# Projection steps spread over attention's rest, and two feed-forward weight pairs begun ahead of the last scale

## The chip, the cores and the metric

The kernel runs on one core of one Trainium2 chip. The metric is the device time of one execution, in microseconds; lower is better. A core has five engines that work at the same time and meet only through semaphores: PE (TensorE, matrix products; its weight loads are listed apart as PEld), DVE (VectorE), ACT (ScalarE), POOL (GpSimd) and SP (SyncE, which here only issues DMA transfers; POOL issues some too). Each engine works its own list of instructions in a fixed order.

## The reference, cut to what matters

The kernel computes one encoder layer for two request groups, a long one of 2048 tokens and a short one of 256, with the same weights. The model width is 1024, the feed-forward width 2816.

```python
h = rmsnorm(x, norm1_w)
p = h @ w_in
mq, mk, mv, mo, gates, aq, ak, av = jnp.split(p, cuts, axis=-1)
m_out = mlstm_mixer(mq, mk, mv, mo, gates, b_gates, mh_norm_w)
a_out = attention_mixer(aq, ak, av, q_norm_w, k_norm_w)
x = x + jnp.concatenate([m_out, a_out], axis=-1) @ w_out
h = rmsnorm(x, norm2_w)
u = centred_dwconv(h @ w_up, conv_w, conv_b)
a, g = jnp.split(u, 2, axis=-1)
return x + (jax.nn.silu(g) * a) @ w_down
```

The change touches the output projection (`@ w_out`), the second norm and the first products of `h @ w_up`.

## The kernel before, in words

Every fp32 operand of a product is split into a high part (an fp32r copy made by ACT) and a low part (the rest, made by DVE's subtraction), and each product is three matmuls: high by high, high by low, low by high. So nearly every operand costs an ACT copy and a DVE subtraction ahead of the matmuls that read it; the low part is read last.

The work runs in four stages. The first (`phase_a`) norms x and projects it. In the second, the mLSTM and the attention run side by side: `run_both` (L1481) holds a generator for each and takes the next step of whichever is behind by cost units. A step of attention scores 256 keys against 512 queries (L553, L554, tiles `ps`), ACT takes the exponent (L557, `pe`) and the high part (L558, `xx`), DVE the low part (L559), and PE multiplies with the values (L570, L571, L572 into `pv`; L572 is the one that reads the low part). The running maxima for the next head come from L530 (`px`) and DVE's L532 (`mx`). At a head pair's end ACT copies `pv` out (L580), DVE takes a reciprocal (L585), POOL multiplies (L586) and stores the outcome to `mix_d` in DRAM (L591).

When the mLSTM is through, `after_m` opens the memory of the third stage, `phase_c` (L906), which is a generator too: four steps that load and split the 16 half tiles of W_out (`wo`), then nine blocks of 256 tokens in the order `ORDER = (0, 1, 2, 3, 4, 5, 8, 6, 7)`, block 8 being the short sequence, each in eight steps. A block loads its mixed heads (`cmx`, L931 to L933), multiplies them with W_out (L945, tiles `po`, 192 matmuls of 256 columns a block), adds the residual (L952, tiles `cx`), squares (L955) and sums (L957, L960). One block later `tail` makes the scale: PE sums over partitions (L129, `rs_c`), DVE adds epsilon (L132, `rcol_c`), POOL takes the power (L133), PE spreads it over the partitions (L135), DVE scales the block in eight instructions (L964) and four DMAs store it to `n2_d` (L966); the last block's four stores go through POOL's queue, the others through SP's. `run_both` takes `CSTEP = 1` step of this generator ahead of every attention step, where the heads that the next block needs have been issued (`g.mixed`). The steps that are left when attention has ended are taken by the loop over `rest` in `body`, with the first loads of the feed-forward between them; the last block's scale is kept for `g.c_end()`.

The feed-forward (`phase_d`) multiplies in a seven-product scheme: for each pair of weight chunks (`UpPair`) the products "11", "21", "t2", "t1", "t3", "22", "t4" of quarter blocks, with sums of the weights (`w_sums`, L1055, tiles `tw`) and sums of the normed tokens (`nt`). "11" (into `pa`) and "21" (into `pb`) read the loaded weights (`wa`), the next two read `wb`, which is split from the sums `tw`. Token operands are loaded and split at L1020 to L1022 (`n`, `nt`): those of "11", "21", "t2" (`EARLY`) in the loop over `rest`, the other four (`LATE`), of two halves each, in `up_phase` at a raised priority, into memory that `wo` and the last `cmx` held. The first group's two pairs are number 22 and number 0: pair 22 has its "11" and "21" issued ahead of `g.c_end()`, pair 0 behind it, in `begin`.

The order of instructions on each engine is not the program's: a scheduler fixes it when the kernel is built, from the program, the priorities and the pools, so an edit of one stage moves instructions of its neighbours too.

## Time and profile before

| | us |
|---|---|
| three runs | 3367.17, 3370.07, 3371.93 |
| median | 3370.07 |
| the profiled execution | 3374.5 |
| its span, first to last instruction | 3372.8 |
| PE busy | 3265.6 (97%) |
| DVE busy | 2449.7 (73%) |
| ACT busy | 1993.7 (59%) |
| mLSTM's last products | about 1446 on the trace's clock |
| attention's last product | 1806.06 |
| last product of the projection | ends by 1868.64 |
| first product of the feed-forward with summed weights | 1890.39 |

A row of the timeline holds the start in us, the duration in us, engine, source line, operation, what it writes and reads, the number of instructions in the row, and in brackets how long the engine had been idle before it and what ended that. Matmuls overlap in the pipeline, so the time a matmul takes of PE is the distance from its start to the next one's start, not its duration. A row of the windows gives the length of a stretch, then for each engine its busy time and its instructions, then the granted TensorE clock (1.00 is full), the share of the DMA engines and what they moved. `PE L945` with `x1309` in a table by lines means 1309 matmuls of that line in the window.

### The profile page before, as it was taken

The page shows a single profiled execution, that of the slowest core. Times are in us where ns is not written, and L with a number is a line of the kernel's source. Part 1 is how long each engine was busy: PE and PEld are TensorE (multiplying, and loading weights), DVE is VectorE, ACT ScalarE, POOL GpSimd, SP SyncE. Part 2 cuts the span into 40 slices and gives each one's busy share as a digit, 9 for nine tenths or more (in the row PEclk, how much of TensorE's full clock was granted, in tenths as well). Part 3 has the DMA queues.
Part 4 walks back from the last instruction along what each step waited for, and adds up shares of the span by engine and source line. Part 5 has one row for each costly group of instructions (what it writes and reads, how often), then busy time and mean ns, then how long its engine had stood idle before and what let it go on. Part 6 is the DMA issues. An engine that isn't in the chain of part 4 may idle for free.

```text
span 3372.8 us, 53440 instructions
## 1 busy us (share of the span) xinstructions
PE 3265.6 (97%) x19566; PEld 3040.0 (90%) x19566; DVE 2449.7 (73%) x3659; ACT 1993.7 (59%) x3706; POOL 689.1 (20%) x1076
## 2 busy tenths in 40 slices
PE   7889999999999999999998899999999999999998
PEld 6778888888888888878887899999999999999998
DVE  7874576667657768876665799998889888666664
ACT  4535666666666766765454555676667667554543
POOL 7774033313225323211111100000000000010101
PEclk9999999999999999999999899999999999999999
DMA  8766243333236434423335666677666657867673
GB/s 245 214 182 180 91 137 94 108 106 112 94 107 206 133 123 129 142 89 107 97 97 175 242 210 218 215 249 263 240 224 240 212 195 262 312 225 276 226 241 117
DMA packets 393783, 601.69 MB, mean 178 GB/s; under 512 B 31248, under 2 KB 254512, under 8 KB 393520
## 3 DMA queue, kind: packets, MB, share of 16 engines
q1 hardware_dynamic: 360144, 552.38, 48.9%
q0 software_dynamic: 11920, 34.09, 3.7%
q10 hardware_dynamic: 21456, 11.80, 1.2%
q8 instruction: 154, 2.52, 0.3%
q14 instruction: 109, 0.89, 0.1%
HBM read 434.23 MB, written 163.92 MB: 177 GB/s over the span
## 4 chain that ended last, share of the span: by engine, by line
PE 55%; DMA 3%; issue 2%; DVE 2%; ACT 2%; POOL 1%; SPq 0%; POOLq 0%; DVEq 0%; ACTq 0%
PE pa L1097 16%; PE pc L1097 8%; PE pf L1354 5%; PE po L945 5%; PE pb L1097 4%; PE ph L1354 3%; PE pg L1354 2%; PE mv L711 1%; PE ps L553 1%; PE ps L554 1%; PE pv L570 1%; PE pv L572 1%; PE pv L571 1%; PE px L530 1%; DMA nt<-act_d 1%
## 5 line engine op out<-in xcount | busy, mean ns | idle before, releaser
L559 DVE TENSOR_TENSOR xx<-pe,xx 128x1024 fp32r<-128x1024 f32 x260 | 320.5, 1234 | 156.3 <-ACT xx L558 155.2
L557 ACT ACTIVATE pe<-ps 128x1024 f32<-128x1024 f32 x260 | 266.1, 1024 | 234.1 <-PE ps L554 227.1
L532 DVE TENSOR_REDUCE mx<-px 128x1 f32<-128x1024 f32 x256 | 310.1, 1218 | 115.4 <-PE px L530 115.0
L1312 POOL TENSOR_TENSOR sq<-sq,sq 128x384 f32<-128x384 f32 x38 | 49.4, 1300 | 1389.5 <-ACT sq L1308 1309.2
L558 ACT ACTIVATE xx<-pe 128x1024 fp32r<-128x1024 f32 x260 | 275.1, 1058 | 5.6
L945 PEld LDWEIGHTS po<-cmx,wo 128*128 128x128 f32 x1728 | 234.6, 193 | 35.2 <-ACT cmx L932 13.5
L945 PE MATMUL po<-cmx,wo 128*128 128x256 f32 x1728 | 243.2, 285 | 14.8 <-ACT cmx L932 12.7
L1101 ACT ACTIVATE u<-pa 128x386 f32<-128x386 f32 (+2 forms) x264 | 129.3, 490 | 174.4 <-PE pa L1097 173.3
L570 PE MATMUL pv<-xx,vv 128*128 128x512 f32 x520 | 212.1, 408 | 7.4 <-ACT xx L558 4.4
L553 PE MATMUL ps<-qq,kk 128*128 128x512 f32 x520 | 214.7, 413 | 4.5 <-ACT pe L557 3.9
L572 PE MATMUL pv<-xx,vv 128*128 128x512 f32 x520 | 210.8, 405 | 1.5 <-DVE xx L559 1.3
L554 PE MATMUL ps<-qm,kl 65*128 65x512 f32 x520 | 208.2, 400 | 0.0
L571 PE MATMUL pv<-xx,vl 128*64 128x512 f32 x520 | 208.2, 400 | 0.0
L685 PEld LDWEIGHTS mj<-mn,wm 128*128 128x128 f32 x1296 | 179.6, 193 | 18.9 <-ACT og L699 4.6
L685 PE MATMUL mj<-mn,wm 128*128 128x256 f32 x1296 | 193.1, 288 | 2.9 <-ACT og L699 2.5
L695 PE MATMUL mv<-wm,mn 128*128 128x256 f32 x1296 | 191.0, 287 | 2.7 <-ACT qb L691 2.5
L695 PEld LDWEIGHTS mv<-wm,mn 128*128 128x128 f32 x1296 | 177.3, 191 | 17.1 <-ACT qb L691 4.0
L227 PE MATMUL pj<-w_a,n1T 128*128 128x512 f32 (+1 forms) x864 | 179.3, 362 | 10.0 <-DVE n1T L185 6.7
L227 PEld LDWEIGHTS pj<-w_a,n1T 128*128 128x128 f32 x864 | 144.6, 196 | 30.1 <-DVE n1T L185 7.6
L530 PE MATMUL px<-kk,qq 128*128 128x512 f32 x512 | 165.6, 405 | 5.1 <-ACT pe L557 3.4
L789 ACT ACTIVATE dm<-dm,tm 128x128 f32<-128x128 f32 x288 | 95.9, 392 | 111.5 <-POOL dm L786 107.0
L1097 PE MATMUL pb<-n,wa 128*128 128x386 f32 (+2 forms) x792 | 147.5, 341 | 3.8 <-DVE cx L964 3.8
(326 smaller groups left out, 8316.1 us busy)
## 6 DMA issues: line engine op xcount, KB each, us to landing
mn<-n_d SPq DMA_DIRECT2D x216, 256.0 KB, 3.3
ru<-w_up SPq DMA_DIRECT2D x88, 512.0 KB, 5.2
rs<-wsu_d SPq DMA_DIRECT2D x88, 512.0 KB, 5.5
act_d<-ts SPq DMA_DIRECT2D x33, 768.0 KB, 5.8
nt<-act_d SPq DMA_DIRECT2D x60, 384.0 KB, 4.9
re_t<-wsd_d SPq DMA_DIRECT2D x45, 512.0 KB, 5.5
wsu_d<-tw SPq DMA_DIRECT2D x44, 512.0 KB, 4.2
act_d<-ya SPq DMA_DIRECT2D x99, 192.0 KB, 2.9
```

The lines of the kernel that those rows point to most:

```text
L227: nc.tensor.matmul(pjs[t][:, c0:c1], nTs[tiles[t]][:, c, a, :], ws[c][:, b, c0:c1], start=(c == 0 and k == 0), stop=(c == NCC - 1 and k == 2))
L532: nc.vector.tensor_reduce(s.mx[:, t0, z0:z0 + 1], ps, AX.X, ALU.max)
L553: nc.tensor.matmul(o, kk[:, kc:kc + P], s.qq, start=True, stop=False)
L557: nc.scalar.activation(pe, ps, AF.Exp)
L558: nc.scalar.activation(x[:, 0], pe, AF.Copy)
L559: nc.vector.tensor_tensor(x[:, 1], pe, f32(x[:, 0]), ALU.subtract)
L570: nc.tensor.matmul(s.pv, vv[:, kt % 4, :], x1, start=kt == 0, stop=False)
L685: nc.tensor.matmul(pj[:, o], s.w[c][:, a, o * P:(o + 1) * P], nT[c][:, h, :], start=(c + o + k == 0), stop=(c == NCC - 1 and k == 2 and o ...
L695: nc.tensor.matmul(pv[:, o], nT[c][:, a, o * P:(o + 1) * P], s.w[c][:, h, 256:512], start=(c + o + k == 0), stop=(c == NCC - 1 and k == 2 ...
L945: nc.tensor.matmul(po[:, o], wo[c][z // 2][:, a, n], mx[c][:, h, :], start=(c == 0 and k == 0), stop=(c == NCC - 1 and k == 2))
L1097: s.nc.tensor.matmul(p, w[:, aa, c, :], ops[k][:, c, bb, 0:s.n], start=c == 0 and i == 0 and not add, stop=c == NCC // 2 - 1 and i == 2, s ...
L1354: nc.tensor.matmul(ps[c], w[:, aa, c, :], t[:, gi - g0, bb, 0:H], start=gi == 0 and m == 0 and not more, stop=gi == NG - 1 and m == 2, ski ...
```

## The change

Three things change.

- `run_both` no longer takes a projection step ahead of every attention step. It counts the attention steps that are left when the mLSTM ends (`left`) and takes steps so that 52 of them (4 of weights and six blocks of eight, `CSTEPS`) are spread evenly over these; it never begins the seventh block of the order, the short sequence's block 8, so that this block's eight steps are issued after attention's last step. 
- The operands of "t1" and "t3" (`MID`) get a pool of their own, `d_m`, in the memory of the W_out halves 4 to 7. Those halves now lie in a stack of their own, which is closed ahead of `g.c_end()`; the loads of `MID` are issued there.
- Pair 0 also has its products "11" and "21" issued ahead of `g.c_end()`, into the same PSUM pool as pair 22's. The third PSUM tile of both pairs (`pc`) comes from the other pool.

Lines of the changed kernel from 81 to about 1480 have numbers that are lower by one: its L944 is L945 here, its L963 is L964.

```diff
-CSTEP = 1
+CSTEPS = 52
...
-EARLY, LATE = OPS[:3], OPS[3:]
+EARLY, MID, LATE = OPS[:3], OPS[3:5], OPS[5:]
...
-        s.g, s.nc, s.s1, s.ps, s.b, s.jj = g, g.nc, s1, ps, b, jj
+        s.g, s.nc, s.s1, s.ps, s.pc, s.b, s.jj = g, g.nc, s1, ps, ps, b, jj
...
-        return s.ps.tile([P, 512], F32, tag="p", name=f"p{k}_{s.nm}", bufs=PB)[:, 0:s.n]
+        return (s.pc if k == "c" else s.ps).tile([P, 512], F32, tag="p", name=f"p{k}_{s.nm}", bufs=PB)[:, 0:s.n]
...
-def phase_d(g, tc, s1, pd, ops, first):
+def phase_d(g, tc, s1, sm, pd, ops, first):
...
-        sl = st.enter_context(tc.tile_pool(name="d_l", bufs=1, side="right", reuse_waits="tile"))
+        sr = st.enter_context(tc.tile_pool(name="d_l", bufs=1, side="right", reuse_waits="tile"))
+        sl = {k: s1 if k in EARLY else sm if k in MID else sr for k in OPS}
...
-    late = n2_ops(sl, 0, LATE)
+    for p in first:
+        p.pc = banks[1]
     with tc.high_priority(offset=APRI):
-        for k, e in zip(LATE, P0):
-            n2_load(g, late, 0, k, engs=e)
-    ops.update(late)
+        for k in LATE:
+            ops.update(n2_ops(sl[k], 0, [k]))
+            n2_load(g, ops, 0, k)
...
     def begin(b, gi):
-        prs = [UpPair(g, s1, banks[0], b, 2 * gi + NFC)] if not first else [first.pop()]
-        prs.append(UpPair(g, s1, banks[1], b, 2 * gi))
-        for k, p in enumerate(prs):
-            if (b, gi, k) != (0, 0, 0):
-                p.mul(p.p1, "11", opsb[b])
-        for k, p in enumerate(prs):
-            if (b, gi, k) != (0, 0, 0):
-                p.second(opsb[b])
+        if (b, gi) == (0, 0):
+            return first
+        prs = [UpPair(g, s1, banks[k], b, 2 * gi + NFC * (1 - k)) for k in range(2)]
+        for p in prs:
+            p.mul(p.p1, "11", opsb[b])
+        for p in prs:
+            p.second(opsb[b])
         return prs
...
-                swo = pool(s_wo, "wo", bufs=1, side="right")
                 sc = pool(s_wo, "c_s", bufs=2, side="right")
                 pc = pool(s_wo, "c_p", bufs=2, space=PSUM, side="right")
+                g.s_sw = s_wo.enter_context(ExitStack())
+                swo = pool(g.s_sw, "wo", bufs=1, side="right")
...
             first[0].second(ops)
+            g.s_sw.close()
+            sm = pool(s2, "d_m", bufs=1)
+            with tc.high_priority(offset=APRI):
+                for k in MID:
+                    ops.update(n2_ops(sm, 0, [k]))
+                    n2_load(g, ops, 0, k)
+            first.append(UpPair(g, s1, pd, 0, 0))
+            first[1].mul(first[1].p1, "11", ops)
+            first[1].second(ops)
             g.c_end()
             s_wo.close()
-            phase_d(g, tc, s1, pd, ops, first)
+            phase_d(g, tc, s1, sm, pd, ops, first)
...
+    na_s, left, steps = 2 * (16 * 8 + 2), 0, 0
...
                 tile_c = next(c)
+                left = max(na_s, 1)
         else:
-            for _ in range(CSTEP):
-                if c is not None and (tile_c is None or tile_c in g.mixed):
-                    tile_c = next(c, NT)
+            if c is not None and steps * left < CSTEPS * (left - na_s) and tile_c != 2 * ORDER[6] and (
+                    tile_c is None or tile_c in g.mixed):
+                tile_c = next(c)
+                steps += 1
...
             da = None if s is None else da + s
+            na_s -= 1
```

The places in the order of instructions on which the prediction rests follow. First PE at the hand-over to the feed-forward, from the projection's last row to the first product with `wb` (`cacc7` and `rs_c7` are block 7's sums of squares, the kernel's last scale); before:

```order
L945 MATMUL po7_3_20911<-cmx7_7_20721,wo7_1_17285 128x256 x3
L1097 MATMUL pa_0_22_20970<-n11_0_20190,wa0_22_20967 128x386 x10
L1097 MATMUL pb_0_22_20983<-n21_0_20191,wa0_22_20967 128x386 x10
L129 MATMUL rs_c7_20997<-ones_82,cacc7_20799 128x2 x2
L135 MATMUL rs_c7_20997<-ident_73,rcol_c7_21000 128x128 x2
L1097 MATMUL pa_0_0_21071<-n11_0_20190,wa0_0_21068 128x386 x12
L1097 MATMUL pb_0_0_21084<-n21_0_20191,wa0_0_21068 128x386 x12
L1097 MATMUL pa_0_22_20970<-nt2_0_20192,wb0_22_21121 128x386 x2
```

After:

```order
L944 MATMUL po7_3_20911<-cmx7_7_20721,wo7_1_17321 128x256 x3
L1096 MATMUL pa_0_22_20970<-n11_0_20076,wa0_22_20967 128x386 x10
L1096 MATMUL pb_0_22_20983<-n21_0_20077,wa0_22_20967 128x386 x10
L1096 MATMUL pa_0_0_21019<-n11_0_20076,wa0_0_21016 128x386 x12
L1096 MATMUL pb_0_0_21032<-n21_0_20077,wa0_0_21016 128x386 x12
L128 MATMUL rs_c7_21046<-ones_82,cacc7_20799 128x2 x2
L134 MATMUL rs_c7_21046<-ident_73,rcol_c7_21049 128x128 x2
L1096 MATMUL pa_0_22_20970<-nt2_0_20078,wb0_22_21124 128x386 x2
```

Pair 0's 24 products have moved ahead of the two rows of the scale's sums. The row of `po7_3` above and the 342 matmuls of L945 from attention's last value product to it are as many as before, all of blocks 6 and 7 after one another; none of block 8 has moved there.

The same place on DVE, from the first split of late operands (`n22`, `nt1`, `nt3`, `nt4`; each row of one is half a tile) to the scale's last rows; before:

```order
L1022 TENSOR_TENSOR nt1_0_21035<-nt1_0_21035 128x2x386
L1104 TENSOR_TENSOR u0_22_21117<-pb_0_22_20983,u0_22_21117 128x386
L132 TENSOR_SCALAR rcol_c7_21000<-rs_c7_20997 128x2
L1022 TENSOR_TENSOR nt1_0_21035<-nt1_0_21035 128x2x386
L1022 TENSOR_TENSOR nt3_0_21036<-nt3_0_21036 128x2x386
L964 SCALAR_TENSOR_TENSOR cx7_0_20689<-cx7_0_20689,nw_84,rs_c7_20997 128x256 x2
L964 SCALAR_TENSOR_TENSOR cx7_1_20690<-cx7_1_20690,nw_84,rs_c7_20997 128x256 x2
L964 SCALAR_TENSOR_TENSOR cx7_2_20691<-cx7_2_20691,nw_84,rs_c7_20997 128x256
L1022 TENSOR_TENSOR nt3_0_21036<-nt3_0_21036 128x2x386
L964 SCALAR_TENSOR_TENSOR cx7_2_20691<-cx7_2_20691,nw_84,rs_c7_20997 128x256
L1022 TENSOR_TENSOR n22_0_21037<-n22_0_21037 128x2x386 x2
L1022 TENSOR_TENSOR nt4_0_21038<-nt4_0_21038 128x2x386
```

After:

```order
L1103 TENSOR_TENSOR u0_22_21120<-pb_0_22_20983,u0_22_21120 128x386
L1021 TENSOR_TENSOR n22_0_21083<-n22_0_21083 128x2x386
L1021 TENSOR_TENSOR nt4_0_21090<-nt4_0_21090 128x2x386
L1021 TENSOR_TENSOR nt1_0_21000<-nt1_0_21000 128x2x386 x2
L1103 TENSOR_TENSOR u0_0_21122<-pb_0_0_21032,u0_0_21122 128x386
L131 TENSOR_SCALAR rcol_c7_21049<-rs_c7_21046 128x2
L1021 TENSOR_TENSOR nt3_0_21007<-nt3_0_21007 128x2x386 x2
L963 SCALAR_TENSOR_TENSOR cx7_0_20689<-cx7_0_20689,nw_84,rs_c7_21046 128x256 x2
L963 SCALAR_TENSOR_TENSOR cx7_1_20690<-cx7_1_20690,nw_84,rs_c7_21046 128x256 x2
L963 SCALAR_TENSOR_TENSOR cx7_2_20691<-cx7_2_20691,nw_84,rs_c7_21046 128x256
L1021 TENSOR_TENSOR nt4_0_21090<-nt4_0_21090 128x2x386
L963 SCALAR_TENSOR_TENSOR cx7_2_20691<-cx7_2_20691,nw_84,rs_c7_21046 128x256
```

L132 (now L131) stood behind one split and one copy of pair 22 (`u0_22`); now five splits (the row ahead of this piece is the first, of `n22`), that copy and pair 0's `u0_0` stand ahead of it. Two more splits follow ahead of the first scale product, as before. Of the eight splits five stood among the scale products; now one does.

The third place is DVE in the middle of attention's rest, where the projection of block 4 (`po4_0`, `po4_1`) waits for the last of its mixed heads (`cmx4_7`) and block 3 is scaled (`cx3`). The tiles `xx4_12` are those of the attention head in work, the next figure numbering its eight passes over the keys (1, 2, 3 here), and `mx5_12` holds the maxima for the head that follows; before:

```order
L559 TENSOR_TENSOR xx4_12_1_18255<-pe4_12_1_18254,xx4_12_1_18255 128x1024
L132 TENSOR_SCALAR rcol_c3_19330<-rs_c3_19327 128x2
L532 TENSOR_REDUCE mx5_12_18195<-px5_12_2_0_18265 128x1
L532 TENSOR_REDUCE mx5_12_18195<-px5_12_3_0_18269 128x1
L964 SCALAR_TENSOR_TENSOR cx3_0_18743<-cx3_0_18743,nw_84,rs_c3_19327 128x256 x2
L964 SCALAR_TENSOR_TENSOR cx3_1_18744<-cx3_1_18744,nw_84,rs_c3_19327 128x256 x2
L964 SCALAR_TENSOR_TENSOR cx3_2_18745<-cx3_2_18745,nw_84,rs_c3_19327 128x256 x2
L933 TENSOR_TENSOR cmx4_7_19243<-cmx4_7_19243 128x256
L964 SCALAR_TENSOR_TENSOR cx3_3_18746<-cx3_3_18746,nw_84,rs_c3_19327 128x256 x2
L532 TENSOR_REDUCE mx5_12_18195<-px5_12_0_1_18360 128x1
L933 TENSOR_TENSOR cmx5_7_19685<-cmx5_7_19685 128x256
L559 TENSOR_TENSOR xx4_12_2_18344<-pe4_12_2_18343,xx4_12_2_18344 128x1024
```

After:

```order
L131 TENSOR_SCALAR rcol_c3_19356<-rs_c3_19353 128x2
L531 TENSOR_REDUCE mx5_12_18170<-px5_12_2_0_18236 128x1
L531 TENSOR_REDUCE mx5_12_18170<-px5_12_3_0_18240 128x1
L558 TENSOR_TENSOR xx4_12_1_18226<-pe4_12_1_18225,xx4_12_1_18226 128x1024
L963 SCALAR_TENSOR_TENSOR cx3_0_18769<-cx3_0_18769,nw_84,rs_c3_19353 128x256 x2
L963 SCALAR_TENSOR_TENSOR cx3_1_18770<-cx3_1_18770,nw_84,rs_c3_19353 128x256 x2
L963 SCALAR_TENSOR_TENSOR cx3_2_18771<-cx3_2_18771,nw_84,rs_c3_19353 128x256 x2
L963 SCALAR_TENSOR_TENSOR cx3_3_18772<-cx3_3_18772,nw_84,rs_c3_19353 128x256 x2
L531 TENSOR_REDUCE mx5_12_18170<-px5_12_0_1_18295 128x1
L558 TENSOR_TENSOR xx4_12_2_18279<-pe4_12_2_18278,xx4_12_2_18279 128x1024
L932 TENSOR_TENSOR cmx4_7_19269<-cmx4_7_19269 128x256
```

The low part of pass 1 stood ahead of the two maxima, now it stands behind them, next to the eight scale products. On PE the same stretch has, before, around the row that spreads the scale (L135):

```order
L571 MATMUL pv4_12_18423<-xx4_12_1_18255,vl1_16_0_10624 64x512
L572 MATMUL pv4_12_18423<-xx4_12_1_18255,vv1_16_0_10623 128x512
L570 MATMUL pv4_12_18423<-xx4_12_1_18255,vv1_16_0_10623 128x512
L571 MATMUL pv4_12_18423<-xx4_12_1_18255,vl1_16_0_10624 64x512
L572 MATMUL pv4_12_18423<-xx4_12_1_18255,vv1_16_0_10623 128x512
L135 MATMUL rs_c3_19327<-ident_73,rcol_c3_19330 128x128 x2
L553 MATMUL ps4_12_2_18338<-qq4_12_17721,kk1_16_4_10632 128x512
L554 MATMUL ps4_12_2_18338<-qm4_12_17723,kl11_16_4_10633 128x512
L553 MATMUL ps4_12_2_18338<-qq4_12_17721,kk1_16_4_10632 128x512
L554 MATMUL ps4_12_2_18338<-qm4_12_17723,kl11_16_4_10633 128x512
L530 MATMUL px5_12_0_1_18360<-kk1_16_8_10643,qq5_12_18191 128x512
L530 MATMUL px5_12_0_1_18360<-kk1_16_12_10654,qq5_12_18191 128x512
```

After, from that row on:

```order
L134 MATMUL rs_c3_19353<-ident_73,rcol_c3_19356 128x128 x2
L552 MATMUL ps4_12_2_18273<-qq4_12_17696,kk1_16_4_10632 128x512
L553 MATMUL ps4_12_2_18273<-qm4_12_17698,kl11_16_4_10633 128x512
L552 MATMUL ps4_12_2_18273<-qq4_12_17696,kk1_16_4_10632 128x512
L553 MATMUL ps4_12_2_18273<-qm4_12_17698,kl11_16_4_10633 128x512
L529 MATMUL px5_12_0_1_18295<-kk1_16_8_10643,qq5_12_18166 128x512
L529 MATMUL px5_12_0_1_18295<-kk1_16_12_10654,qq5_12_18166 128x512
L571 MATMUL pv4_12_18374<-xx4_12_1_18226,vv1_16_0_10623 128x512
L569 MATMUL pv4_12_18374<-xx4_12_1_18226,vv1_16_0_10623 128x512
L570 MATMUL pv4_12_18374<-xx4_12_1_18226,vl1_16_0_10624 64x512
L571 MATMUL pv4_12_18374<-xx4_12_1_18226,vv1_16_0_10623 128x512
L552 MATMUL ps4_12_3_18364<-qq4_12_17696,kk1_16_4_10632 128x512
```

The first product with the low part of pass 1 (L571 on `xx4_12_1`; L572 before) now stands behind that row; the matmuls of the projection that stood between such rows before are all issued further ahead, so that from the row of block 3's sums (L128, 17 rows ahead of this piece) to the row of `po4_0` with `cmx4_7` only attention is left. At attention's end DVE has the eight scale products of block 8 between the low parts of the last head's passes 6 and 7; before they stood ahead of that of pass 3.

9 lines of the change are left out of this document (4 added, 5 removed).

## The prediction

> **What bounds the kernel now.** First the busy times by stretch from attention's rest to the feed-forward (length, then busy us and instructions of PE, PEld, DVE, ACT, POOL, then clock).
>
> ```profile
> 1640.00:1660.00 20.00, 19.23 (x118) 16.40 (x117) 18.20 (x30) 12.79 (x21) 5.38 (x6) 1.00 0.38 118
> 1870.00:1890.00 20.00, 11.46 (x46) 10.26 (x44) 15.36 (x26) 9.78 (x14) 6.34 (x7) 0.73 0.67 230
> ```
>
> PE is the bound through attention's rest: even this worst stretch of it, 1640 to 1660, lacks only 0.77 us, at clock 1.00. Around the last scale, 1870 to 1890, it is half empty, and behind attention's end there is a hole that the timeline shows below. Only such holes can be won, and the change touches both. Is the full stretch full of work, or of waiting that counts as busy? The groups of PE by line, 1480 to 1806 (0.8 us of idle in all):
>
> ```profile
> L945 PE MATMUL po<-cmx,wo 128*128 128x256 f32 x1309 | 185.8, 281 | 0.4 <-ACT cmx L932 0.4
> L572 PE MATMUL pv<-xx,vv 128*128 128x512 f32 x119 | 47.1, 396 | 0.0
> ...
> L553 PE MATMUL ps<-qq,kk 128*128 128x512 f32 x116 | 46.5, 400 | 0.4 <-ACT pe L557 0.4
> ...
> L530 PE MATMUL px<-kk,qq 128*128 128x512 f32 x96 | 30.0, 396 | 0.0
> ```
>
> L570 and L571 have L572's count, L554 L553's. The timeline shows what each takes of PE: the distance of starts (24 of 256 columns lead by 2.88 us to the next row, 0.12 each; 512 columns 0.2335 in a dense run).
>
> ```profile
> 1795.09 0.39 PE L570 MATMUL pv<-xx,vv 128*128 128x512 f32 x1
> 1795.32 0.39 PE L571 MATMUL pv<-xx,vl 128*64 128x512 f32 x1
> ...
> 1865.76 3.04 PE L945 MATMUL po<-cmx,wo 128*128 128x256 f32 x24
> 1868.64 1.92 PE L1097 MATMUL pa<-n,wa 128*128 128x386 f32 x10
> 1870.40 1.93 PE L1097 MATMUL pb<-n,wa 128*128 128x386 f32 x10
> 1872.48 0.61 PE L129 MATMUL rs_c<-ones,cacc 128*128 128x2 f32 x4 [0.16 <-POOL cacc L960]
> 1875.87 1.22 PE L135 MATMUL rs_c<-ident,rcol_c 128*128 128x128 f32 x4 [2.78 <-POOL rcol_c L133]
> 1876.74 3.46 PE L1097 MATMUL pa<-n,wa 128*128 128x386 f32 x12
> 1883.99 4.20 PE L1097 MATMUL pb<-n,wa 128*128 128x386 f32 x12 [3.79 <-DVE cx L964]
> 1890.39 1.01 PE L1097 MATMUL pa<-nt,wb 128*128 128x386 f32 x2 [2.21 <-ACT wb L1069]
> ```
>
> 1309 × 0.12 = 157 and (3 × 119 + 2 × 116 + 96) × 0.2335 = 160, together 317 of 326 us; the small products of scales and transposes are most of the other 9. Spreading matmuls inside a full stretch wins nothing.
>
> **The spread: the hole behind attention.** The first projection row behind attention's last product:
>
> ```profile
> 1818.75 6.42 PE L945 MATMUL po<-cmx,wo 128*128 128x256 f32 x30 [12.29 <-ACT cmx L932]
> ```
>
> It holds 12.29 us, the way of the last head pair through ACT, DVE, POOL, DRAM and back. Block 8 needs none of that, and its 192 matmuls would be 23 us of cover. But it is only issued after attention, and the scheduler still decides where it stands: in the order of the changed kernel PE has 342 matmuls of L945 behind attention's last product, as before, those of blocks 6 and 7; block 8 has been moved up among attention's last heads. The hole stays: 0.
>
> **The spread: inside attention's rest.** Its effect is one of order. Where PE waits for block 4's last heads, before it has a few projection matmuls between passes; after only attention, with block 3's eight scale products on DVE in the same place.
>
> ```profile
> 1649.50 0.50 PE L129 MATMUL rs_c<-ones,cacc 128*128 128x2 f32 x4
> 1649.86 0.71 PE L530 MATMUL px<-kk,qq 128*128 128x512 f32 x2
> ...
> 1655.11 0.51 PE L945 MATMUL po<-cmx,wo 128*128 128x256 f32 x2 [0.37 <-ACT cmx L932]
> 1656.02 0.50 PE L553 MATMUL ps<-qq,kk 128*128 128x512 f32 x1 [0.41 <-ACT pe L557]
> ```
>
> The same stretch on DVE:
>
> ```profile
> 1651.01 2.34 DVE L532 TENSOR_REDUCE mx<-px 128x1 f32<-128x1024 f32 x2
> 1653.38 2.44 DVE L964 SCALAR_TENSOR_TENSOR cx<-cx,nw,rs_c 128x256 f32<-128x256 f32 x6
> ...
> 1658.32 2.36 DVE L559 TENSOR_TENSOR xx<-pe,xx 128x1024 fp32r<-128x1024 f32 x2
> ```
>
> A maximum costs DVE 1.17, a low part 1.18, a scale product 0.41. Count from block 3's sums row in the new order. PE: the sums 0.36, then twelve products of 512 columns (2.80) to the end of the next head's first maximum, 3.2; there DVE makes two maxima and the low part of pass 1: 3.2 + 2.3 + 1.2 = 6.7. PE has four more such products (0.93), the spread row 0.4 and six (1.40) until it wants that low part: 5.9, so it waits 0.8. Then DVE scales (3.25), makes a maximum and the low part of pass 2: 12.3. PE has 16 products and two of 256 columns, 4.0, and stands at 10.7: it waits 1.6. Together 2.4, less the 0.78 that the idle brackets above show for today: **+1.6**. Bounds: 0 if the scheduler's reordering is as harmless as today's, +3.2 if block 4's last heads come late as well, by another two of today's waits.
>
> At attention's end block 8's scale now stands between the low parts of the last two passes. Counted from the end of pass 6's scores, PE has 29 products of 512 columns, 12 of 256 and the scale's spread row until it wants the low part of pass 7: 6.8 + 1.4 + 0.4 = 8.6. The spread row is through at 4.5 (17 of 512 columns, one of 256, itself); from there DVE needs 8 × 0.41 and the low part's 1.18, so 9.0 and a hand-over of 0.2. **+0.6**, between 0 and +1.2 (twice that).
>
> At the start, 1440 to 1480, PE waits for the first weights and heads. The spread takes its steps a little later there, and the order of the waits stays alike. 0, between -1.1 and +1.1, a wait like the one of this row, whose trail comes in again below:
>
> ```profile
> 1424.87 0.95 PE L530 MATMUL px<-kk,qq 128*128 128x512 f32 x2 [1.11 <-ACT pe L557]
> 1425.62 0.63 PE L553 MATMUL ps<-qq,kk 128*128 128x512 f32 x1
> 1426.05 0.63 PE L554 MATMUL ps<-qm,kl 65*128 65x512 f32 x1
> ...
> 1428.61 0.41 PE L572 MATMUL pv<-xx,vv 128*128 128x512 f32 x1
> ```
>
> **The pairs begun early.** Pair 0's 24 products move from behind the last scale's sums to ahead of them. They take 24 × 0.176 = 4.2 us of PE at full clock (ten of pair 22's lead by 1.76, 1868.64 to 1870.40). Before they lay in the wait for `wb`, which ends at 1890.39 whatever they do, pair 0's being through at 1888.2. So moving them saves nothing there, and it delays the scale, on which the path runs. The rows of DVE, ACT and POOL on it:
>
> ```profile
> 1874.24 0.15 DVE L132 TENSOR_SCALAR rcol_c<-rs_c 128x2 f32<-128x2 f32 x1
> 1877.13 2.05 DVE L964 SCALAR_TENSOR_TENSOR cx<-cx,nw,rs_c 128x256 f32<-128x256 f32 x5 [0.41 <-PE rs_c L135]
> ...
> 1882.98 0.86 DVE L964 SCALAR_TENSOR_TENSOR cx<-cx,nw,rs_c 128x256 f32<-128x256 f32 x2
> 1886.75 0.69 DVE L1055 TENSOR_TENSOR tw<-ru 128x512 f32<-128x512 f32 x1 [0.84 <-DVE tw L1055]
> 1888.57 0.68 DVE L1055 TENSOR_TENSOR tw<-tw,ru 128x512 f32<-128x512 f32 x1
> ```
>
> ACT's third and fifth split of late operands, and the split of `wb`:
>
> ```profile
> 1874.88 0.85 ACT L1021 ACTIVATE nt<-nt 128x772 fp32r<-128x772 f32 x1 [0.95 <-DMA nt<-n2t_d]
> ...
> 1876.97 0.85 ACT L1021 ACTIVATE n<-n 128x772 fp32r<-128x772 f32 x1 [0.20 <-DMA n<-n_d]
> ...
> 1889.29 2.26 ACT L1069 ACTIVATE wb<-tw 128x1024 fp32r<-128x1024 f32 x2 [6.13 <-DVE tw L1055]
> ```
>
> And POOL's power:
>
> ```profile
> 1874.47 1.35 POOL L133 TENSOR_TENSOR rcol_c<-rcol_c,mhalf 128x2 f32<-128x2 f32 x1 [2.03 <-DVE rcol_c L132]
> ```
>
> A sums tile shares memory with the last scaled block, so the `tw` at 1886.75 waits for the landing of that block's last store, 2.9 us behind the last scale product (1883.84); the bracket names DVE, which had long been done. Step by step after: pair 22 is through at 1870.40 + 1.76, pair 0 at 1876.4, and the sums row follows (before 1872.48). L132 then stands behind five splits, paced by their DMAs (1.04 each, 1874.88 to 1876.97 for two): the fifth high part is ready at 1877.8, its low part a split (0.95) later, pair 0's copy 0.5: 1879.3. Power 1.4, spread row, 1.26 from spread to scale as before: 1882.1 for 1877.13. Eight scale products, 3.3, with one split (0.9) among them instead of five: the last ends at 1886.3; the splits that stood there are done earlier, which wins back 2.5 of the 5.0 lost. Landing 1889.1; then five DVE rows of 0.6 to the first sum for `wb` where before four stood (the tiles have changed places, and the second of them now shares that memory), and 1.1 of ACT: 1893.4 for 1890.39, **+3.0**. Bounds: +0.9 if no split holds L132 or the scale (scale from 1880.0, last at 1884.2), +4.0 with one more gap between DMAs like ACT's 0.95 at 1874.88. The new pool for "t1" and "t3" doesn't help: its memory comes free with the same last matmul of the projection, since every `po` reads W_out's last chunk.
>
> **Sum**: 0 + 1.6 + 0.6 + 0 + 3.0 = +5.2 us. On the profiled execution 3374.5 becomes 3379.7; that run was 4.4 above the median, so against 3370.07 I say 3375.3. 0.2%, about what a measurement can tell from no change, is 6.7 us: same, on the slow side.
>
> **Rivals.** *Slower: the clock.* A wait of PE may cost twice, since the clock can fall after it. For it: behind the wait at 1424.87 the products came 0.43 apart until 1428.61, nine of them in 3.74 us instead of 2.1, 1.6 us more. Against, a longer wait with no such trail:
>
> ```profile
> 893.13 0.50 PE L570 MATMUL pv<-xx,vv 128*128 128x512 f32 x1 [1.88 <-ACT xx L558]
> 893.47 0.39 PE L571 MATMUL pv<-xx,vl 128*64 128x512 f32 x1
> 893.70 0.38 PE L745 MATMUL mt<-ident,mkT 128*128 128x128 f32 x2
> ```
>
> If both new waits of the middle stretch cost it, +3.2 comes on top: +8.4, 3378.5. It decides from one such trail on (5.2 + 1.6 = 6.8). [...] Chance 0.28.
>
> *Faster: block 8 covers the hole after all.* 12.29 us of matmuls, and no slow restart (30 in 6.42 us instead of 3.6, so 2.8): 5.2 - 15.1 = -9.9, 3360.2. For: block 8's steps are issued behind attention. Against: PE works in order, and the order has nothing of block 8 there. A second way to the same side I don't see. 0.10.
>
> *Nothing reaches the path.* The waits in the middle are taken up by slack that I counted as full, and no split holds L132: 0.9 in all, 3371.0. For it speaks that today's order has the same eight products in the same stretch and waits 0.78. 0.17.
>
> **Numbers.** My sum has the remaining 0.45, of which 0.07 lies above 6.7 where its upper bounds meet (1.6 more in the middle, 0.6 at the end, 1.0 at the hand-over: up to +8.4). So faster 0.10, same 0.38 + 0.17 = 0.55, slower 0.28 + 0.07 = 0.35. The range leaves out the hole's filling and the top of the rest: from 3366 (the sum with all lower bounds, 0.9 - 1.1 = -0.2, the runs' own spread, 2.9 below their median, and one more for terms I didn't see) to 3381 (+8.4, their spread upward, 1.9, and a little).
>
> **What would show it.** Right: an idle of about 12 us on PE between attention's last product and L945; none of block 8's rows in it; two waits near 1.6 and 0.8 on the low part L558 in the middle; at the hand-over the sums row about 4 us later, the restart with `wb` about 3 us later against the last projection. Wrong: PE busy in that hole; a restart no later than before; matmuls at 0.43 after the waits.

## The result, and the profile after

The changed kernel takes 3376.39 us in the median (3371.44 to 3384.70) where the kernel before takes 3370.72 in the runs beside it. The ratio is 1.0019, with a 95% interval of 1.0011 to 1.0027, so 3.7 to 9.1 us slower. The profiled execution of after took 3372.21 us, at the fast end of its runs; it shows where the time lies, stage against stage, and says nothing on the total.

The timeline of PE in the middle stretch and at attention's end, with the two waits that were forecast for the first and the hole behind the second:

```profile
1647.98 0.50 PE L571 MATMUL pv<-xx,vv 128*128 128x512 f32 x1 [0.35 <-DVE xx L558]
...
1651.98 0.73 PE L529 MATMUL px<-kk,qq 128*128 128x512 f32 x2 [1.14 <-ACT pe L556]
1652.54 0.40 PE L552 MATMUL ps<-qq,kk 128*128 128x512 f32 x1
1652.78 0.39 PE L553 MATMUL ps<-qm,kl 65*128 65x512 f32 x1
...
1800.45 0.50 PE L571 MATMUL pv<-xx,vv 128*128 128x512 f32 x1 [0.37 <-DVE xx L558]
...
1813.98 16.25 PE L944 MATMUL po<-cmx,wo 128*128 128x256 f32 x114 [12.34 <-ACT cmx L931]
```

The two waits sum to 1.49 us where today's pair had 0.78. The second is not on a low part: a maximum's product (L529) waits for ACT's exponent. From 1652.54 on the rows stand 0.24 apart, not 0.43: no trail of slow products. The hole holds 12.34 us (12.29 before).

PE at the hand-over, from pair 22's first product to the first one with `wb`:

```profile
1862.46 1.95 PE L1096 MATMUL pa<-n,wa 128*128 128x386 f32 x10
1864.25 1.93 PE L1096 MATMUL pb<-n,wa 128*128 128x386 f32 x10
1866.01 2.30 PE L1096 MATMUL pa<-n,wa 128*128 128x386 f32 x12
1868.15 2.28 PE L1096 MATMUL pb<-n,wa 128*128 128x386 f32 x12
1870.27 0.50 PE L128 MATMUL rs_c<-ones,cacc 128*128 128x2 f32 x4
1874.40 1.22 PE L134 MATMUL rs_c<-ident,rcol_c 128*128 128x128 f32 x4 [3.62 <-POOL rcol_c L132]
1887.07 1.01 PE L1096 MATMUL pa<-nt,wb 128*128 128x386 f32 x2 [11.45 <-ACT wb L1068]
```

From pair 22's start to the sums it is 7.81 us (before 1872.48 - 1868.64 = 3.84), and to the first product with `wb` 24.61 (before 1890.39 - 1868.64 = 21.75): 2.86 more. Why, the same stretch on DVE shows:

```profile
1871.42 0.96 DVE L1021 TENSOR_TENSOR nt<-nt 128x772 fp32r<-128x772 f32 x1 [0.36 <-ACT nt L1020]
1872.30 0.55 DVE L1103 TENSOR_TENSOR u<-pb,u 128x386 f32<-128x386 f32 x1
1872.77 0.15 DVE L131 TENSOR_SCALAR rcol_c<-rs_c 128x2 f32<-128x2 f32 x1
1872.83 1.82 DVE L1021 TENSOR_TENSOR nt<-nt 128x772 fp32r<-128x772 f32 x2
1875.66 2.04 DVE L963 SCALAR_TENSOR_TENSOR cx<-cx,nw,rs_c 128x256 f32<-128x256 f32 x5 [1.00 <-PE rs_c L134]
1877.62 0.95 DVE L1021 TENSOR_TENSOR nt<-nt 128x772 fp32r<-128x772 f32 x1
1878.49 1.25 DVE L963 SCALAR_TENSOR_TENSOR cx<-cx,nw,rs_c 128x256 f32<-128x256 f32 x3
...
1882.83 0.69 DVE L1054 TENSOR_TENSOR tw<-ru,ru 128x512 f32<-128x512 f32 x1 [2.47 <-DMA n_d<-cx]
```

The sums row was through at 1870.8 (1870.27 + 0.50), but L131 ran at 1872.77, behind a split (1871.42) and pair 0's copy (1872.30). Once the scale starts, one split stands among its eight products; before there were four, and a fifth behind the last product. And the bracket at 1882.83 now names the store of the scaled block, for which the prediction had to argue: the sums' tile waits for `n_d<-cx` to land.

### The profile page after: what moved, and what is told of

It is laid out like the page before. It is cut to its first block, busy times and chain, and to the rows that moved or that the text cites. A ratio compares the mean times of both kernels' runs of the same rounds, so it can differ in the third digit from the quotient of the medians.

```text
span 3370.5 us, 53442 instructions
## 1 busy us (share of the span) xinstructions
PE 3256.2 (97%) x19566; PEld 3031.7 (90%) x19566; DVE 2445.5 (73%) x3659; ACT 1994.6 (59%) x3706; POOL 688.4 (20%) x1076
## 4 chain that ended last, share of the span: by engine, by line
PE 53%; DMA 3%; DVE 3%; issue 3%; ACT 2%; POOL 1%; SPq 0%; POOLq 0%; DVEq 0%; ACTq 0%
PE pa L1096 16%; PE pc L1096 8%; PE po L944 6%; PE pf L1354 6%; PE pb L1096 4%; PE ph L1354 2%; PE pg L1354 2%; PE mv L710 1%; PE ps L552 1%; PE ps L553 1%; PE pv L571 1%; PE pv L569 1%; PE pv L570 1%; PE px L529 1%; DMA n<-act_d 1%
## 5 line engine op out<-in xcount | busy, mean ns | idle before, releaser
L944 PEld LDWEIGHTS po<-cmx,wo 128*128 128x128 f32 x1728 | 234.1, 193 | 32.9 <-ACT cmx L931 13.0
L944 PE MATMUL po<-cmx,wo 128*128 128x256 f32 x1728 | 242.2, 285 | 13.9 <-ACT cmx L931 12.3
L571 PE MATMUL pv<-xx,vv 128*128 128x512 f32 x520 | 209.7, 403 | 2.8 <-DVE xx L558 2.6
L226 PE MATMUL pj<-w_a,n1T 128*128 128x512 f32 (+1 forms) x864 | 180.6, 364 | 10.7 <-DVE n1T L184 7.4
L529 PE MATMUL px<-kk,qq 128*128 128x512 f32 x512 | 164.2, 403 | 6.4 <-ACT pe L556 5.1
L1096 PE MATMUL pa<-nt,wb 128*128 128x386 f32 (+2 forms) x792 | 147.4, 340 | 11.4 <-ACT wb L1068 11.4
```

Of the source, the lines that this page charges most:

```text
L226: nc.tensor.matmul(pjs[t][:, c0:c1], nTs[tiles[t]][:, c, a, :], ws[c][:, b, c0:c1], start=(c == 0 and k == 0), stop=(c == NCC - 1 and k == 2))
L944: nc.tensor.matmul(po[:, o], wo[c][z // 2][:, a, n], mx[c][:, h, :], start=(c == 0 and k == 0), stop=(c == NCC - 1 and k == 2))
L1096: s.nc.tensor.matmul(p, w[:, aa, c, :], ops[k][:, c, bb, 0:s.n], start=c == 0 and i == 0 and not add, stop=c == NCC // 2 - 1 and i == 2, s ...
```

## The experiments

All times beside runs of the kernel before on the same chip; ratios are to it, with 95% intervals.

| kernel | median us | ratio | interval |
|---|---|---|---|
| e1_spread | 3375.31 | 1.0005 | 0.9996 to 1.0015 |
| e2_pairs | 3379.12 | 1.0025 | 1.0015 to 1.0035 |
| e3_scale_first | 3380.20 | 1.0021 | 1.0012 to 1.0031 |
| e4_gate | 3382.02 | 1.0032 | 1.0021 to 1.0044 |
| e5_sums_ahead | 3367.32 | 0.9989 | 0.9980 to 0.9997 |
| e7_wo_place | 3372.26 | 0.9999 | 0.9990 to 1.0008 |
| e8_pair_only | 3373.82 | 1.0007 | 0.9997 to 1.0016 |
| e9_gate_half | 3370.01 | 0.9994 | 0.9984 to 1.0004 |
| e10_gate_aligned | 3371.43 | 0.9999 | 0.9988 to 1.0010 |
| e11_sums_shifted | 3375.46 | 1.0011 | 1.0001 to 1.0021 |
| e12_before_gate | 3372.08 | 1.0001 | 0.9992 to 1.0010 |
| e13_gate_no_tile | 3361.17 | 0.9965 | 0.9951 to 0.9978 |

Single profiles of one order of instructions wander: before and e1, and after and e2, lie 4.4 and 5.9 us apart at POOL's first power of a projection block's scale (near 1515), and the stretch from POOL's first power of the down projection (L133, L132 in after; near 3005) to the end differs by 2.6 and 6.0. So stages are compared, and a stage's gain is believed when the time shows it.

### Which part costs what

**e1_spread** is the kernel before with the spread alone.

```diff
-CSTEP = 1
+CSTEPS = 52
...
-            for _ in range(CSTEP):
-                if c is not None and (tile_c is None or tile_c in g.mixed):
-                    tile_c = next(c, NT)
+            if c is not None and steps * left < CSTEPS * (left - na_s) and tile_c != 2 * ORDER[6] and (
+                    tile_c is None or tile_c in g.mixed):
+                tile_c = next(c)
+                steps += 1
```

> The spread alone, with the hand-over to the feed-forward as in the kernel before. My theory (order: two short waits on PE in the middle of attention's rest and one at its end, 0.7 + 0.4 us more idle than before in the changed kernel's trace; the hand-over costs apart): +1 to +2 us against the kernel before, the idle behind attention 12.3 us, the way from the last projection product to the first product with wb 21.7 us as before. Rival (the spread is what costs, by the clock or by its weights coming late): +5 us or more, with the hand-over still 21.7 us. Rival (block 8 covers the hole once the pairs stay put): -8 us, the idle behind attention gone.

The scheduler gives every engine the same list as before, with the same waits and addresses: the spread, alone, does nothing, and this run is a repeat of the kernel before (1.0005).

**e2_pairs** is the changed kernel with the old step rule (`CSTEP = 1`), the inverse edit.

> Pair 0 and the operands of t1 and t3 begun early, one projection step ahead of every attention step as before. My theory (pair 0 on PE and the splits on DVE delay the last scale): +3 us against the kernel before; from the last projection product to the first product with wb 24.6 us for 21.7, the scale's sums row 7.8 us behind the first for 3.8. Rival (the hand-over is free, since it lies in a wait): 0, and 21.7 us.

Its lists are those of after, and it is slower than before by as much (1.0025 for 1.0019, the intervals overlap). So the spread takes no part in the result, and something else in the change reorders attention's rest.

**e7_wo_place** is the kernel before with the pool of W_out opened behind the two pools of the projection, as after has it.

```diff
-                swo = pool(s_wo, "wo", bufs=1, side="right")
                 sc = pool(s_wo, "c_s", bufs=2, side="right")
                 pc = pool(s_wo, "c_p", bufs=2, space=PSUM, side="right")
+                swo = pool(s_wo, "wo", bufs=1, side="right")
```

> The kernel before, with the pool of W_out's second half taken behind the third stage's other pools instead of ahead of them, and nothing else. My theory (this move of memory alone, and not the spread, is what changes the order in attention's rest): PE's idle there as in the changed kernel, two waits of 0.4 and 1.1 us in the middle and 0.4 at the end, hand-over 21.8 us as before: +1 to +2 us against the kernel before. Rival (the hand-over is not alone in costing, the rest loses more): +4 or more.

This line of memory layout gives PE the order of after up to the hand-over, with the two waits in the middle of attention's rest, here 0.24 and 1.00 in the timeline of PE:

```profile
1653.94 0.50 PE L572 MATMUL pv<-xx,vv 128*128 128x512 f32 x1 [0.24 <-DVE xx L559]
...
1657.93 0.72 PE L530 MATMUL px<-kk,qq 128*128 128x512 f32 x2 [1.00 <-ACT pe L557]
```

The time is that of before, 0.9999 (0.9990 to 1.0008): waits that sum to 0.5 us more than before's cannot be told from nothing here.

**e8_pair_only** is the kernel before with pair 0's "11" and "21" issued ahead of the last scale, and the pools as before.

```diff
             first[0].second(ops)
+            first.append(UpPair(g, s1, pd, 0, 0))
+            first[1].mul(first[1].p1, "11", ops)
+            first[1].second(ops)
             g.c_end()
```

> The kernel before, with pair 0's first two products issued ahead of the last scale as in the changed kernel, and every pool where it was. My theory: attention's rest as before, hand-over 24 to 25 us for 21.8, +3 us against the kernel before, the greater part of the change's loss. Rival (the loss comes from the pools): 0.

Up to the hand-over its order is that of before; there PE shows:

```profile
1858.81 1.92 PE L1097 MATMUL pa<-n,wa 128*128 128x386 f32 x10
...
1866.59 0.50 PE L129 MATMUL rs_c<-ones,cacc 128*128 128x2 f32 x4
1870.34 1.22 PE L135 MATMUL rs_c<-ident,rcol_c 128*128 128x128 f32 x4 [3.25 <-POOL rcol_c L133]
1882.38 1.01 PE L1097 MATMUL pa<-nt,wb 128*128 128x386 f32 x2 [10.82 <-ACT wb L1069]
```

1882.38 - 1858.81 = 23.57 us from pair 22's start to `wb`: +1.82 from the pair alone. How far one profile can be trusted here, the repeats tell: 21.75 and 22.11 for before and e1, 24.61 and 24.93 for after and e2. (e7, with W_out's pool moved and pair 0 left where it was, has 1889.13 - 1868.85 = 20.28.) The time, 1.0007 (0.9997 to 1.0016), is higher by 2.4 us, near those 1.8, but not surely. The early pair loses at the hand-over, whatever the pools are; that it carries the whole of the 2.86 in after isn't shown.

### The hand-over

**e3_scale_first** is after with the last scale at a higher priority than the splits of late operands.

```diff
-            g.c_end()
+            with tc.high_priority(offset=3 * APRI):
+                g.c_end()
```

> The changed kernel with the last scale at a priority above the late operands' loads. My theory (what costs is the scale standing behind pair 0 and behind five splits): the sums row, L132 and the scale move ahead, the scale starts about 4.5 us behind the sums as soon as POOL has added the squares, its eight products run without splits among them, so the restart with wb comes about 18.8 us behind the last projection product for 24.6: -6 us against the changed kernel, -1 to 0 against the kernel before. Rival (the late operands' loads set the restart whatever the scale does): 24 to 25 us, no gain.

DVE, from L131 to the scale:

```profile
1878.25 0.15 DVE L131 TENSOR_SCALAR rcol_c<-rs_c 128x2 f32<-128x2 f32 x1
1878.32 0.55 DVE L1103 TENSOR_TENSOR u<-pb,u 128x386 f32<-128x386 f32 x1
1878.79 1.83 DVE L1021 TENSOR_TENSOR nt<-nt 128x772 fp32r<-128x772 f32 x2
1880.53 3.22 DVE L963 SCALAR_TENSOR_TENSOR cx<-cx,nw,rs_c 128x256 f32<-128x256 f32 x8
```

The scale is in one piece, yet L131 still stands behind five splits. Pair 22 starts at 1868.80 here, so L131 runs 9.45 us behind it, for 10.31 in after, and the restart with `wb` comes at 1891.42, 22.62 behind it: 2.0 less than after, a third of what I expected. The time doesn't show them (1.0021).

**e5_sums_ahead** is after with the first half of the weight sums of both pairs, and its split into `wb`, issued ahead of the last scale, into a pool (`d_m`) that shares no memory with the scaled block. All late operands are in one pool again.

```diff
             g.s_sw.close()
-            sm = pool(s2, "d_m", bufs=1)
-            with tc.high_priority(offset=APRI):
-                for k in MID:
-                    ops.update(n2_ops(sm, 0, [k]))
-                    n2_load(g, ops, 0, k)
+            s_sm = s2.enter_context(ExitStack())
+            sm = pool(s_sm, "d_m", bufs=1)
+            first[0].ahead(sm)
             first.append(UpPair(g, s1, pd, 0, 0))
             first[1].mul(first[1].p1, "11", ops)
             first[1].second(ops)
+            first[1].ahead(sm)
             g.c_end()
...
+    def ahead(s, pool):
...
+        s.x = pool.tile([P, D], F32, tag="sum", name=f"tw0_{s.nm}", bufs=SMB)
+        nc.vector.tensor_tensor(s.x[:, h:D], s.r2[:, 0:h], s.r2[:, h:D], ALU.add)
+        nc.vector.tensor_tensor(s.x[:, 0:h], s.x[:, h:D], s.r1[:, 0:h], ALU.subtract)
...
+        s.w.update(zip(("t2", "t1"), split_w(g, s.s1, s.x, "b" + s.nm)))
```

> The changed kernel, with the first half of the weight sums of pairs 22 and 0 and their split (wb) issued ahead of the last scale too, in tiles that share no memory with the scaled block; t1 and t3 lose their own pool for it. My theory (what ends last at the hand-over is the wait of a sums tile for the landing of the scale's last store, so that beginning the pairs wins nothing by itself): PE goes on from pair 0 to wb without that wait; idle from the last projection product to the dense run falls from 17 us to under 8: -8 to -11 us against the changed kernel, -2 to -6 against the kernel before. Rival (DVE is the bound there, whatever waits for the store): the idle only changes its place, 0 against the changed kernel.

PE has its first products with `wb` 1887.25 - 1870.54 = 16.71 us behind pair 22's start, without a wait:

```profile
1870.54 1.95 PE L1096 MATMUL pa<-n,wa 128*128 128x386 f32 x10
1872.32 1.93 PE L1096 MATMUL pb<-n,wa 128*128 128x386 f32 x10
1875.18 0.61 PE L128 MATMUL rs_c<-ones,cacc 128*128 128x2 f32 x4 [0.93 <-POOL cacc L959]
1878.71 1.01 PE L1096 MATMUL pa<-n,wa 128*128 128x386 f32 x2 [2.92 <-ACT wa L1068]
1879.52 0.85 PE L1096 MATMUL pb<-n,wa 128*128 128x386 f32 x2
1880.16 1.06 PE L134 MATMUL rs_c<-ident,rcol_c 128*128 128x128 f32 x4
1882.22 3.42 PE L1096 MATMUL pa<-n,wa 128*128 128x386 f32 x10 [1.00 <-DVE wa L1069]
1885.48 1.93 PE L1096 MATMUL pb<-n,wa 128*128 128x386 f32 x10
1887.25 2.29 PE L1096 MATMUL pc<-nt,wb 128*128 128x386 f32 x12
```

That is 7.9 less than after, and the time follows: 0.9989 (0.9980 to 0.9997), faster than before, and 0.3% below after's 1.0019, 9 us by the medians and 10 by the ratios. The two kernels differ in two things, though. Pair 0 is issued early here too, but the scheduler has put all 24 of its products behind the row of the scale's sums (1875.18), 20 of them behind the scale's spread (1880.16). The kernel before, whose pair 0 stands behind both, is the nearer comparison: 21.75 us there, 16.71 here, 5.0 less.

What set `wb` in before and after was the chain that the prediction named, from the scale over the landing of its store to the weight sums. In e5 the scale's last product ends 19.65 us behind pair 22's start (15.20 before, so 4.4 later), and `wb` comes 5.0 earlier all the same: a late scale no longer holds it. What an early pair 0 costs without that chain no run shows.

### The hole

The prediction priced the hole at a gain, should block 8 stand in it. To put it there, its products are made to depend on the last head.

**e4_gate** is after, and block 8's first mixed tile gets one column rewritten by a copy that reads a value of the last exponent (the column is then loaded over).

```diff
+        if s is last[0] and kp == s.nk // 2 - 1:
+            nc.gpsimd.tensor_copy(g.gate, pe[:, 0:1])
...
+                if b == ORDER[6] and c == 0:
+                    nc.gpsimd.tensor_copy(m[:, 1, 0:1], g.gate)
...
+        g.gate = kp.tile([P, 1], F32, name="gate")
```

> The changed kernel, with block 8's first mixed head made to wait for the last exponent of attention, by a copy of one column from that tile through a small tile (block 8 can't be moved up among attention's last heads any more). My theory (the hole behind attention is real idle time, and the change missed it because the scheduler moved block 8 up): PE works in the hole, its idle there falls from 12.3 to under 3 us, and the restart behind it is at full clock: -9 to -14 us against the changed kernel, -4 to -9 against the kernel before. Rival (what is taken from attention's last heads opens as large a hole among them): idle on exponents and low parts there of 8 us or more, 0 in all.

The hole is gone; the first rows of L951 behind attention wait 1.13 and 1.03 us. But now the last heads lack the 192 matmuls that filled their waits, and the timeline of PE has, among others:

```profile
1743.28 0.50 PE L572 MATMUL pv<-xx,vv 128*128 128x512 f32 x1 [1.37 <-ACT xx L560]
...
1757.78 0.50 PE L574 MATMUL pv<-xx,vv 128*128 128x512 f32 x1 [1.82 <-DVE xx L561]
...
1792.17 8.60 PE L951 MATMUL po<-cmx,wo 128*128 128x256 f32 x70 [1.13 <-DVE cmx L939]
```

From 1480 to 1790 PE idles 7.6 us where after had 1.5. The time is worse, 1.0032, and these waits alone don't explain it, since the hole's 12.34 are won.

**e9_gate_half** is e5 with half of block 8 held back, so that the other half stays with the last heads: a one-column copy into the PSUM tile of its third group of products, ahead of them.

```diff
+        if b == ORDER[6] and z == 2:
+            nc.vector.tensor_copy(po[:, 0, 0:1], g.gate)
```

> The kernel with the sums ahead, and the second half of block 8's projection (96 matmuls, 11.4 us) made to wait for attention's last exponent by a copy of one column into its PSUM tile. My theory (the hole behind attention can be covered if only as much is held back as fills it): the idle there falls from 12.3 to under 2 us, at 1 to 4 us more idle among attention's last heads: -6 to -12 us against the kernel with the sums ahead, the fastest of all. Rival (what is held back is missed among the last heads as much as it wins behind them, as the gate on the whole block looked): 0 to -3.

In the profile it does what it should: the first projection product behind attention waits 1.35 us, a later one 4.00, and from POOL's power for block 5 (L132), where both still have one order, to `wb` it takes 129.5 us where e5 takes 135.8, 6.3 less. Yet the time is not lower (0.9994 for e5's 0.9989). Either the gain is lost where I hadn't looked, or the edit costs something far from its place. The gate's four bytes lie among the constants, and the allocator moved the tiles of the first stage, of attention and most of those of the feed-forward by 32 bytes (in e4 as well); those of the mLSTM and of the projection kept their places.

**e10_gate_aligned** has the gate at 64 bytes (`kp.tile([P, 16], F32, ...)`), **e11_sums_shifted** is e5 with no gate and an unused 4-byte tile among the constants, and **e12_before_gate** is the kernel before with e10's gate and no other edit.

> The kernel of e9_gate_half with one tile changed: the gate tile has 16 columns of f32 (64 bytes a partition) instead of one, so every tile behind it keeps the address that it has in e5_sums_ahead; the order of the instructions is e9's. In e9 the last po ended 12.4 us earlier after attention's end than in e5 (profiles: idle 0 and 1.35 for 12.37) and the first product of wb came 10.4 us earlier from the same start, yet the time was 3370.0 for 3367.3. Theory A (the gate's 4 bytes shifted the tiles that follow, and the shift costs elsewhere what the hole gave): 3355 to 3360 us, 8 to 12 below e5. Theory B (the shift is harmless; what e9 gained in the hole is lost again behind it, at a bound that comes later whatever attention's end does): about 3370, like e9. In both the profile's idle between attention's last product and L944's next is under 2 us, and a busy total of PE before 1440 us like before's.

> The kernel of e5_sums_ahead with a 4-byte tile, set once by POOL, among the constants, so that nearly all tiles stand 32 bytes off; the order of PE, DVE, ACT and SP is e5's. Theory A (the shift costs): 4 to 12 us above e5, 3371 to 3379, and some group of instructions longer in the profile than in e5's. Theory B (the shift is harmless): 3367.3 within the interval of half a part in a thousand, 3365 to 3370.

> The kernel before with one thing added: the second half of block 8's products (96 of 256 columns, 11.5 us of PE) waits for the last head pair's exponent of the last pass but none, by a one-column copy into its PSUM tile, so that they stand in the hole behind attention; the gate tile is 64 bytes, so addresses move by multiples of 64. My account of the hole (12.29 us of idle that only such work can fill): the idle falls under 2 us and the time by 6 to 12 us, 3359 to 3365. Rival (the path behind attention is set by something that does not come earlier when the hole is filled, such as a DMA or POOL chain of the feed-forward): idle gone, the time 3369 to 3372 as before.

e11 agreed with the theory of the addresses: with e5's order and tiles elsewhere it is at 1.0011 (1.0001 to 1.0021) for 0.9989. e10 and e12 spoke against it as I had put it, 64 bytes harmless: both fill the hole, e12 with waits of 2.29 and 5.65 in the place of 12.29, and both take the time of before. What decided was the table of DMA issues over the first 60 us (transfers, KB each, median us to landing), here e5, then e11, then e10:

```profile
n_d<-n1T SPq DMA_DIRECT2D x4, 1024.0 KB, 5.2
...
q_d<-qz SPq DMA_DIRECT2D x1, 512.0 KB, 3.8
```

```profile
n_d<-n1T SPq DMA_DIRECT2D x4, 1024.0 KB, 6.2
...
q_d<-qz SPq DMA_DIRECT2D x1, 512.0 KB, 5.2
```

```profile
n_d<-n1T SPq DMA_DIRECT2D x4, 1024.0 KB, 6.3
...
q_d<-qz SPq DMA_DIRECT2D x1, 512.0 KB, 5.3
```

The stores from SBUF take a fifth longer (1 MB) and more than a third longer (512 KB) in both, and in e4, e9 and e12 as well (6.2 to 6.3, 5.1 to 5.2), while before, after, e1 and e5 have 5.2 to 5.3 and 3.8 to 4.1. So a tile of 64 bytes shifts too, and the test left is one that moves nothing.

**e13_gate_no_tile** is e10 without the gate's tile: the copy into PSUM reads the exponent itself.

```diff
-            nc.gpsimd.tensor_copy(g.gate[:, 0:1], pe[:, 0:1])
+            g.gate = pe
...
-        g.gate = kp.tile([P, 16], F32, name="gate")
```

> The kernel of e10_gate_aligned without its gate tile: the one-column copy into the PSUM tile reads the exponent itself, POOL's copy goes, every tile stands at the address that it has in e5_sums_ahead, and the order of PE, DVE, ACT and SP is e10's. In the profiles so far the stores of the first 60 us take longer in each kernel with a tile more among the constants, 4 bytes or 64 (n_d<-n1T 6.2 to 6.3 us to landing for 5.2 to 5.3, q_d<-qz 5.1 to 5.3 for 3.8 to 4.1), whatever its order, and PE waits 1.15 us for the sums near 58 us where it waited 0.2. Theory A (the new addresses cost about 3 us at the start, and more later through the same stores, and so ate what the hole gave): stores back at 5.2 and 3.8 to 4.1, hole filled, time 3358 to 3364, 4 to 9 below e5 and 8 to 12 below e10. Theory B (the addresses' cost does not reach the end, and the hole's gain is lost behind attention): stores back as well, but time 3367 to 3371.

Theory A's time came: 3361.17 us, ratio 0.9965 (0.9951 to 0.9978), every run of it below every run of the kernel before beside it. PE's order is e10's. e10 in the timeline of PE, at the first row of `pr` (made from attention's first maxima) and in the down projection:

```profile
266.61 0.64 PE L543 MATMUL pr<-identr,m4r 128*128 128x128 f32 x4
...
3168.00 1.44 PE L128 MATMUL rs_d<-ones,sq 128*128 128x2 f32 x6 [4.35 <-POOL sq L1339]
```

e13 in the same places, and behind attention:

```profile
263.30 0.64 PE L543 MATMUL pr<-identr,m4r 128*128 128x128 f32 x4
...
1807.74 4.06 PE L951 MATMUL po<-cmx,wo 128*128 128x256 f32 x32 [1.67 <-ACT cmx L936]
...
1835.02 8.58 PE L951 MATMUL po<-cmx,wo 128*128 128x256 f32 x48 [5.21 <-DVE cx L958]
...
1876.05 1.22 PE L134 MATMUL rs_c<-ident,rcol_c 128*128 128x128 f32 x4 [5.64 <-POOL rcol_c L132]
...
3164.39 0.83 PE L128 MATMUL rs_d<-ones,sq 128*128 128x2 f32 x6 [1.18 <-POOL sq L1339]
```

e13 is 3.3 us ahead of e10 at the first row, 2.5 at the first product with `wb` (1882.84 for 1885.38), but 0.4 at POOL's first power of the down projection (2999.26 for 2999.63), 3.6 at the wait near 3164 and 7.7 at the end of the spans (3363.1 for 3370.8). Its stores land in 5.3 and 4.2 us. So nearly all of the difference between these two profiles arises in the down projection, and the slower stores at the start aren't shown to be its cause.

The hole's 12.37 us (e5) became 1.67, and part of it came back as 5.21 at 1835.02: PE is through with the products ahead of that place at 1829.8, some 12 us earlier than at the like place in e5 (1842.0), and the add on DVE that it waits for (L958) stands behind sums of tokens (L1047) that waited 2.32, 1.13 and 1.16 us for their loads. Another part came back at 1876.05, where PE waits for POOL's power of the last scale:

```profile
1869.77 6.23 POOL L132 TENSOR_TENSOR rcol_c<-rcol_c,mhalf 128x2 f32<-128x2 f32 x1 [4.25 <-DVE rcol_c L131]
```

It takes 6.23 us here and in e10, where PE waits the same 5.64 for it, and 1.35 in before and in after; why isn't known. So from POOL's power for block 5 to `wb` e13 takes 135.1 us, e5 135.8, e9 129.5: in e13's profile, the slowest of its five runs, the filled hole hardly shows. What shows is the time: by the medians the half gate is worth 6.2 us on top of e5 (3361.17 for 3367.32), by the ratios 8 (0.9965 for 0.9989, intervals apart by 0.0002). The kernel beats before and after.

## Why the prediction was right

**The sum.** Forecast 0 + 1.6 + 0.6 + 0 + 3.0 = +5.2, "same, on the slow side". The two profiles have +0.05 at the hole, +0.71 in the middle (1.49 for 0.78), +0.37 at attention's end, +2.86 at the hand-over, together 4.0. The medians differ by 5.7, with 4.0 inside the interval of 3.7 to 9.1. That 5.2 and 5.7 lie so close is in part luck: the forecast has 0.9 too much in the middle, and the profiles leave 1.7 of the medians' difference without a place. Of the 0.6 forecast at attention's end, 0.2 was a hand-over between engines that no run shows: in after the product at 1800.45 starts 0.06 behind the end of the low part that it waits for (1799.17 + 1.22).

**The hole** held, 12.34 us, and none of block 8's rows stood in it.

**The hand-over** came term by term, counted from pair 22's start: sums at 7.8 (forecast 7.8), L131 at 10.3 (10.7), the first scale product at 13.2 (13.5), the last one's end at 17.3 (17.7), the sum behind the landed store at 20.4 (20.5), `wb` at 24.6 (24.8). e8 shows that pair 0's place alone brings 1.8 of the 2.9, e5 that `wb` hung on the scale by the way over the store's landing. One count was off without changing a sum: among the scale products stood four splits before, not five.

**The middle stretch** failed in two ways. The step "the spread: inside attention's rest. Its effect is one of order" had the right order and the wrong cause: e1 and e2 show the spread to move nothing at all, and e7 the place of W_out's pool to move everything. The prediction read the order of the changed kernel and gave the effect to the edit that spoke of order. And the size was too high, 0.71 for 1.6. The forecast 0.8 and 1.6 on two low parts became 0.35 on a low part and 1.14 on an exponent. Ten products of 512 columns and two of 256 behind the first wait, PE came to a maximum's product, six products ahead of the low part that was to hold it, and that product was let go by ACT's exponent; the low part was then there in time. Without that hold PE would have waited for it by an estimated 1.1 us: six products of 0.2335 from 1650.84 on bring PE to 1652.2, and the low part was through at 1653.3.

**The rival of the clock** fell: the rows behind the wait of 1.14 us stand 0.24 apart from 1652.54 on, and the granted clock is 1.00 from 1648 to 1660. The trail at 1424.87, nine products 0.43 apart behind a wait of 1.11, was the clock: in before it is 0.50 from 1425.2 to 1428.6, and 1.00 from 1421.8 to 1425.2 and from 1428.6 to 1432.0. But a wait of that length alone doesn't bring it on: behind the 1.14 in after, and behind the 1.88 at 893.13 in before, where the clock is 1.00 from 893 to 897, no trail follows.

**The rival of the covered hole** was rightly unlikely for this change, but its price was too high: 15.1 us forecast, while e13 gains 6 to 8 from it. The prediction counted PE's idle as won outright; work moved into the hole is taken from waits behind it (5.21 at 1835.02) and ahead of it (1480 to 1790: 3.7 us of idle in e13, 2.4 in e5).

**What stays open.** Whether the move of W_out's pool costs the 0.5 us that its waits say: too small for these runs. What after's new pool for "t1" and "t3" does by itself: not tried alone, so it may hold a part of the loss that e8 (1.0007) leaves of 1.0019. Why POOL's last power took 6.23 us in e10 and e13. How the addresses cost their time: from POOL's first power of the down projection to the end e4, e9, e10 and e11 take 368.7 to 371.2 us and most others 362.9 to 367.7, but e12, shifted as well, takes 364.3, and e2, not shifted, 370.9; the wait of 4 us there follows the same pattern (3.99 to 4.35, 0.15 in e12, 3.71 in e2).
